# A two-layer decoder trunk in split FP32 on one core: separate banks for one product of the value projection, and another order for its operand sums

## The chip, the cores and the metric

The kernel runs on one core of a Trainium2 chip. The metric is the device time of one launch in microseconds (us). Engines are named as the profile names them: PE multiplies matrices (PEld is its weight load), DVE is the vector engine, ACT the scalar engine, POOL and SP issue DMAs among other things. Every engine works through its own list of instructions in order. PE writes into eight accumulator banks of 128 x 512 FP32, which only DVE and ACT empty.

## The reference

Two post-norm layers; each is one input projection of 512 tokens, three groups of attention heads, gates, an output projection and a layer norm. Cut to what matters:

```python
def hybrid_layer(x, mem, w_in, b_forget, w_mem_kv, w_out, ln_gain, ln_bias):
    h = jnp.einsum('bsd,dn->bsn', x, w_in)            # 512 x 2048 times 2048 x 8278
    (fq, fk, fv, fg, f_logit, dq, dk, dv, dg, iq, ik, iw, mq, mg) = jnp.split(h, offsets, axis=-1)
    cum_logf = jnp.cumsum(jax.nn.log_sigmoid(f_logit + b_forget), axis=1)
    y_fox = fox_attention(heads(fq), heads(fk), heads(fv), cum_logf) * jax.nn.silu(fg)
    # dsa: an indexer scores all keys of a query, the best 128 are kept
    y_dsa = dsa_attention(rope(heads(dq), pos), rope(heads(dk), pos), heads(dv),
                          q_idx, k_idx, w_idx) * jax.nn.silu(dg)
    y_mem = memory_attention(heads(mq), k_mem, v_mem) * jax.nn.silu(mg)
    y = jnp.einsum('bsn,nd->bsd', jnp.concatenate([y_fox, y_dsa, y_mem], axis=-1), w_out)
    return layer_norm(ALPHA * x + y, ln_gain, ln_bias)
```

All arrays are FP32. The change concerns how `fv`, `dv`, `fg` and `dg` (3072 columns of `h`) are computed, and when the best 128 keys are picked.

## The kernel before, in words

**Products.** A number is held as a first part `hi`, rounded by ACT to the format that PE multiplies fast, and a second part `lo = x - hi`, made by DVE (`split`, lines 197 to 199). A product is three matmuls: hi x hi, lo x hi, hi x lo (lines 205 to 207).

**Weights.** They arrive in chunks of 128 x 2048 (1 MB) in three buffers `raw`. A chunk is used in two half-steps. `split_w` turns half a chunk into `whi` (ACT, line 198) and `wlo` (DVE, line 199); there are four buffers of each. At half-step n the program splits the half that half-step n+3 needs, so `whi` of n+3 takes the buffer that PE frees at the end of half-step n-1.

**The value stage.** The 3072 value and gate columns are computed for three pairs of 512-column blocks. For each pair there are seven products in place of eight block products (Strassen's scheme in Winograd's form). The left operands are blocks of x (A11, A12, A22) or sums of them (S1 to S4); the right ones are weight blocks or sums of these (T1 to T4), which lie ready in DRAM, or are made by a DMA that adds a block to a chunk in place (`grow_w`, line 234). A product has two chunks (g = 0 and 1), so four half-steps of twelve matmuls. In each layer first come P1, P7, P2, Q6 and Q4 for the pairs 0, 1 and 2 (`VAL_FIRST`, P2 in two parts around Q6), then Q5 and Q3 for all three (`VAL_SECOND`).

A product accumulates in two banks (for the token halves st = 0 and 1). P1, P7, Q6 and Q4 of a pair share the two banks of chain "a", one accumulating on the other, P2 has chain "b", and Q5 and Q3 share chain "c". When a product's last half-step is issued, `val_out` takes out what stands in its banks: after P1 a copy M1 (ACT, line 804); after P7 the difference to M1, M7 (DVE, line 807); after P2 M1 plus the bank (DVE, line 810); after Q6 minus the bank (ACT, line 814) and M7 minus the bank (DVE, line 817); after Q4, Q5 and Q3 a copy (ACT, line 821). The results go to DRAM by DMAs that POOL issues.

**Operand sums.** `val_operands` is a generator that makes S3 and S2 early, and then waits until the last P7 is through. It then makes S1 for the four feature tiles i = 0 to 3, waits for the last Q6, and makes S4. The sum S2 itself is dropped once it is split (the split holds -S2); so for each tile of S1 or S4 line 767 adds its two parts up again, four additions on half tiles (line 731) bring in the two parts of the x block, ACT makes the first part `vxh` (line 736), and after one yield DVE makes the second part `vxl` (line 741).

**What sets the order.** The program is written out in the order in which the engines get it. A list `active` holds generators like `val_operands`; `tick` resumes each once after a half-step, and those begun with `whole=True` only after a chunk while the value stage runs. In the attention heads all of them go on after each half.

**Key choice.** `top_keys` picks 128 keys a query in 48 rounds on DVE (lines 604 and 605: the largest eight, then strike them out), two rounds a step; 16 rounds each for 256, 384 and 512 keys. It is begun when the last Q6 is issued, and goes on in the rest of the value stage and the first heads. The DSA heads, six heads later, need its result.

Of the kernel before, what the change touches and what calls it, by code (L numbers as in the profile page):

```python
# [70 lines left out]
VAL_FIRST = (("P1", 0), ("P1", 1), ("P7", 0), ("P7", 1), ("P2", 0), ("Q6", 0), ("Q6", 1), ("P2", 1),  # L71
             ("Q4", 0), ("Q4", 1))
VAL_SECOND = (("Q5", 0), ("Q5", 1), ("Q3", 0), ("Q3", 1))
VAL_CHAIN = {"P1": "a", "P7": "a", "Q6": "a", "Q4": "a", "P2": "b", "Q5": "c", "Q3": "c"}
VAL_OPENS = ("P1", "P2", "Q5")
GROWN = {"Q6": ("P7", (0, 0)), "Q4": ("Q6", (1, 0))}


# [79 lines left out]
def kernel(  # L158
# [244 lines left out]

    kmem, vmem, gates, qs, ks, vs = {}, {}, {}, {}, {}, {}
    ys, left = {}, {}
    masks = {}

    def gate(key, ps):

# [187 lines left out]
    def top_keys(l):  # L597
        acc = masks[l]
        for qb in (1, 2, 3):
            b, off, w = PACK[qb]  # L600
            a = acc[b][:, off:off + w]
            for n in range(TOPK // 8):
                m8 = small("m8", 8)
                nc.vector.max(m8, a)
                nc.vector.match_replace(out=a, in_to_replace=m8, in_values=a, imm_value=TAKEN)
                if n % 2:
                    yield 1 + n // 2 % 2 if now[1] == "heads" else 1

            nc.vector.tensor_scalar(a, a, TAKEN / 2, NEG, op0=ALU.is_gt, op1=ALU.mult)

    def attend(l, kind, h):
        key = (kind, h)
# [130 lines left out]
    def val_operands():  # L743
        add, sub = ALU.add, ALU.subtract
        a11, a12, a21, a22 = (0, 0), (0, 1), (1, 0), (1, 1)

        for i in range(4):
            val_sum("S3", i, ((a11, 0, add), (a21, 0, sub), (a11, 1, add), (a21, 1, sub)))
            yield 1
        for i in range(4):  # L750
            val_hi("S3", i)
            val_sum("S2", i, (("S3", 0, add), (a22, 0, add), (a22, 1, add)))
            yield 1
            val_lo("S3", i)
            yield 1
        for i in range(4):
            hi, lo = vleft["S2", i] = slot("vxh", F32R), slot("vxl", F32R)
            nc.scalar.activation(hi, vx["S2", i], AF.Copy, scale=-1.0)
            yield 1
            nc.vector.scalar_tensor_tensor(lo, vx.pop(("S2", i)), -1.0, hi.bitcast(F32),  # L760
                                           op0=ALU.mult, op1=ALU.subtract)
        for name, a, after in (("S1", a11, "P7"), ("S4", a12, "Q6")):
            yield from wait_for(after)
            for i in range(4):
                t = vx["-S2", i] = slot("vx")
                hi, lo = vleft["S2", i] if name == "S1" else minus.pop(i)
                nc.vector.tensor_tensor(t, hi.bitcast(F32), lo.bitcast(F32), op=add)
                val_sum(name, i, (("-S2", 0, add), (a, 0, add), (a, 1, add)), vx.pop(("-S2", i)))
                val_hi(name, i)
                yield 1  # L770
                val_lo(name, i)
            yield 1

    val_done, minus = [], {}

    def wait_for(name):

# [12 lines left out]
    def val_out(name, pair, ps):  # L790


        if pair == PAIRS - 1:
            val_done.append(name)
            for k in [k for k in vleft if k[0] == PRODUCTS[name][1]]:
                operand = vleft.pop(k)
                if name == "Q6":
                    minus[k[1]] = operand
        j = 2 * pair
        for st in range(2):  # L800
            m1, m7 = ("M1", pair, st), ("M7", pair, st)
            if name == "P1":
                vraw[m1] = slot("vraw")
                nc.scalar.activation(vraw[m1], ps[st], AF.Copy)
            elif name == "P7":
                vraw[m7] = slot("vraw")
                nc.vector.tensor_tensor(vraw[m7], ps[st], vraw[m1], op=ALU.subtract)
            elif name == "P2":
                d = vraw.pop(m1)
                nc.vector.tensor_tensor(d, d, ps[st], op=ALU.add)  # L810
                begin(store_v(d, (j, st)), 1)
            elif name == "Q6":
                d = slot("vraw")
                nc.scalar.activation(d, ps[st], AF.Copy, scale=-1.0)
                begin(store_v(d, (j + 1, 2 + st)), 1)
                d = vraw.pop(m7)
                nc.vector.tensor_tensor(d, d, ps[st], op=ALU.subtract)
                begin(store_v(d, (j + 1, st)), 1)
            else:
                d = slot("vraw")  # L820
                nc.scalar.activation(d, ps[st], AF.Copy)
                key = {"Q4": (j, 2 + st), "Q5": (j + 1, 2 + st), "Q3": (j + 1, st)}[name]
                begin(store_v(d, key, name != "Q4"), 1)

    def store_v(t, key, add=False):
        if add:
# [183 lines left out]
    for i, (kind, l, j, col, _) in enumerate(chunks):  # L1010
# [122 lines left out]
        elif kind == "vs":  # L1133
            if col == 1:
                val_out(name, pair, zs)
                if name in ("Q4", "P2", "Q3"):
                    del chains[VAL_CHAIN[name], pair], zs
        elif kind == "small":
            sm = slot("sm")
            nc.scalar.activation(sm, ps, AF.Copy)  # L1140
            r = slice(96, 96 + H_FOX)
            nc.scalar.activation(sm[r], ps[r], AF.Identity, bias=bfc[r, l:l + 1])
            t = index_rope(ps, 64, 0, nc.vector)
            kh2, kl2 = slot("kh2", F32R), slot("kl2", F32R)
            for r in (0, 64):
                nc.scalar.activation(kh2[r:r + 64], t[:64], AF.Copy)
                nc.vector.tensor_tensor(kl2[r:r + 64], t[:64], kh2.bitcast(F32)[:64],
                                        op=ALU.subtract)
            idx["k"] = (kh2, kl2)
            begin(small_work(l, sm))  # L1150
            if l > 0:
                begin(residual_rows(l), last=True)
        elif kind == "iq":
            t = index_rope(ps, P, P, nc.gpsimd)

            for e in range(2):
                s = slot("iqs", F32R)
                r, o = (slice(0, 64), slice(64, 128)) if e == 0 else (slice(64, 128), slice(0, 64))
                c = slice(P, SEQ)
                nc.scalar.activation(s[r, c], t[r, c], AF.Copy)  # L1160
                nc.vector.tensor_tensor(s[o, c], t[r, c], s.bitcast(F32)[r, c], op=ALU.subtract)
                idx["q", 2 * j + e] = s
            if j == 3:
                begin(index_scores(l), 2, last=True, but="vs")
# [12 lines left out]
            now = (l, "values")  # L1177
        if kind == "mg" and j == 0:
            begin(val_operands(), 2, last=True)
        if kind == "vs" and (name, pair, col) == ("Q6", PAIRS - 1, 1):  # L1180
            begin(top_keys(l), whole=True)
        if kind == "vs" and (name, pair, col) == ("Q3", PAIRS - 1, 1):
            chains.clear()
# [113 lines left out]
```

## Time and profile before

| | |
|---|---|
| median of 3 runs | 1982.84 us (1982.15 to 1982.87) |
| profiled execution | 1982.03 us |
| its span, first to last instruction | 1980.2 us |
| PE busy | 1935.7 us, 98% |
| DVE busy | 1367.2 us, 69% |
| ACT busy | 940.8 us, 48% |
| POOL busy | 315.0 us, 16% |
| HBM traffic | 284 GB/s over the span |

The page's slices show PE at nine tenths or more nearly everywhere. A slice is 49.5 us, so a wait of 1 to 3 us is lost in it. The views that matter are the list of PE's waits, the busy time in stretches of equal work (a stretch is given as from:to in us from the span's start, then its length, then busy time and instructions of each engine, the granted PE clock, and the share and rate of the DMA engines), and the instructions in order of time. A few per cent of the matmul records can be missing, and a stretch counts the instructions that cross its edges.

### The profile page before, as it was taken

How to read it: one execution, taken by the hardware profiler on the slowest of the kernel's cores; microseconds unless marked ns; L12 is line 12 of the kernel's file. 1: busy time of each engine (PE TensorE's matmuls, PEld its weight loads, DVE VectorE, ACT ScalarE, POOL GpSimd, SP SyncE). 2: the span in 40 equal slices, each digit the busy share in tenths (PEclk: the TensorE clock that was granted, in tenths of full speed). 3: DMA queues.
4: the chain of work that ended last, by engine and by line, in shares of the span. 5: the costliest groups of instructions: out<-in, count | busy, mean ns of one | idle time of the engine just before them, and what ended most of it. 6: DMA issues, size and time to landing. Idle time of an engine off the chain costs nothing.

```text
span 1980.2 us, 25263 instructions
## 1 busy us (share of the span) xinstructions
PE 1935.7 (98%) x9314; PEld 1639.5 (83%) x9314; DVE 1367.2 (69%) x2291; ACT 940.8 (48%) x1510; POOL 315.0 (16%) x551
## 2 busy tenths in 40 slices
PE   9999999979999999999999999999799999999997
PEld 8998888858888888888899988887588888888886
DVE  6666664578664567778886877655887645667788
ACT  6564454334343444455475644443443444345452
POOL 0121111111122110110142301110112212002101
PEclk9999999989999999999999999999899999999999
DMA  9568788748786667788889953886596866668856
GB/s 370 199 204 248 214 220 225 212 150 255 239 208 184 182 181 253 209 313 308 247 259 349 257 168 119 220 233 165 178 260 225 212 205 181 169 232 248 308 211 153
DMA packets 88057, 444.21 MB, mean 224 GB/s; under 512 B 11504, under 2 KB 23792, under 8 KB 49404
## 3 DMA queue, kind: packets, MB, share of 16 engines
q0 software_dynamic: 27872, 184.59, 37.9%
q1 hardware_dynamic: 60060, 257.99, 36.1%
q8 instruction: 73, 1.20, 0.2%
q14 instruction: 52, 0.43, 0.1%
HBM read 411.06 MB, written 151.02 MB: 284 GB/s over the span
## 4 chain that ended last, share of the span: by engine, by line
PE 90%; DVE 5%; ACT 2%; issue 1%; DMA 0%; SPq 0%; POOL 0%; DVEq 0%; ACTq 0%; POOLq 0%
PE c L207 15%; PE c L205 15%; PE c L206 15%; PE v L206 7%; PE v L207 7%; PE v L205 7%; PE z L206 5%; PE z L205 5%; PE z L207 5%; PE pt L650 1%; ACT whi L198 1%; DVE wlo L199 1%; DVE vx L731 1%; PE po L207 1%; PE po L206 1%
## 5 line engine op out<-in xcount | busy, mean ns | idle before, releaser
L199 DVE TENSOR_TENSOR wlo<-raw,whi 128x1024 fp32r<-128x1024 f32 (+1 forms) x473 | 581.7, 1234 | 275.8 <-ACT whi L198 269.3
L198 ACT ACTIVATE whi<-raw 128x1024 fp32r<-128x1024 f32 (+1 forms) x473 | 495.5, 1053 | 316.6 <-PE v L207 166.1
L205 PE MATMUL c<-xh,whi 128*128 128x512 f32 (+1 forms) x1312 | 502.5, 383 | 0.0
L207 PE MATMUL c<-xh,wlo 128*128 128x512 f32 (+1 forms) x1312 | 498.3, 380 | 0.0
L206 PE MATMUL c<-xl,whi 128*128 128x512 f32 (+1 forms) x1312 | 496.9, 379 | 0.0
L207 PEld LDWEIGHTS c<-xh,wlo 128*128 128x128 f32 x1312 | 246.2, 188 | 42.7
L206 PEld LDWEIGHTS c<-xl,whi 128*128 128x128 f32 x1312 | 246.6, 188 | 40.5
L205 PEld LDWEIGHTS c<-xh,whi 128*128 128x128 f32 x1312 | 246.4, 188 | 39.8
L327 POOL TENSOR_TENSOR seen<-mark,mhalf 128x1 f32<-128x1 f32 x112 | 36.9, 329 | 871.9 <-DVE mark L326 848.9
L206 PE MATMUL z<-wlo,yh 128*128 128x512 f32 (+1 forms) x434 | 167.8, 387 | 1.2 <-DVE wlo L199 1.2
L205 PE MATMUL z<-whi,yh 128*128 128x512 f32 (+1 forms) x434 | 168.1, 387 | 0.0
L207 PE MATMUL z<-whi,yl 128*128 128x512 f32 (+1 forms) x434 | 167.7, 386 | 0.0
L205 PE MATMUL v<-whi,vxh 128*128 128x512 f32 x384 | 150.3, 391 | 5.5 <-ACT whi L198 3.4
L206 PE MATMUL v<-wlo,vxh 128*128 128x512 f32 x384 | 150.3, 391 | 4.9 <-DVE wlo L199 4.9
L207 PE MATMUL v<-whi,vxl 128*128 128x512 f32 x384 | 149.4, 389 | 0.0
L205 PE MATMUL v<-whi,xh 128*128 128x512 f32 x288 | 117.5, 408 | 13.3 <-ACT whi L198 13.3
L206 PE MATMUL v<-wlo,xh 128*128 128x512 f32 x288 | 117.3, 407 | 5.5 <-DVE wlo L199 5.5
L207 PE MATMUL v<-whi,xl 128*128 128x512 f32 x288 | 116.8, 405 | 0.0
L206 PEld LDWEIGHTS z<-wlo,yh 128*128 128x128 f32 x434 | 81.6, 188 | 18.1 <-DVE wlo L199 2.1
L207 PEld LDWEIGHTS z<-whi,yl 128*128 128x128 f32 x434 | 81.5, 188 | 16.6
L205 PEld LDWEIGHTS z<-whi,yh 128*128 128x128 f32 x434 | 81.5, 188 | 16.3
L206 PEld LDWEIGHTS v<-wlo,vxh 128*128 128x128 f32 x384 | 72.1, 188 | 22.8 <-DVE wlo L199 8.2
(208 smaller groups left out, 2895.9 us busy)
## 6 DMA issues: line engine op xcount, KB each, us to landing
raw<-in_wall_dram SPq DMA_DIRECT2D x155, 1024.0 KB, 7.2
sum<-in_wall_dram POOLq DMA_DIRECT2D x56, 1024.0 KB, 9.7
raw<-sum SPq DMA_DIRECT2D x56, 1024.0 KB, 6.3
raw<-in_wall_dram POOLq DMA_DIRECT2D x24, 1024.0 KB, 8.0
v<-vraw POOLq DMA_DIRECT2D x72, 256.0 KB, 5.2
x<-z POOLq DMA_DIRECT2D x32, 256.0 KB, 9.6
vraw<-v SPq DMA_DIRECT2D x96, 64.0 KB, 5.4
vraw<-v SPq DMA_DIRECT2D x24, 256.0 KB, 6.7
```

Source lines behind the costliest of these rows:

```text
L198: nc.scalar.activation(hi, src, AF.Copy)
L199: nc.vector.tensor_tensor(lo, src, hi.bitcast(F32), op=ALU.subtract)
L205: nc.tensor.matmul(ps, ah, bh, start=start, stop=False, skip_group_check=more)
L206: nc.tensor.matmul(ps, ah, bl, start=False, stop=False, skip_group_check=more)
L207: nc.tensor.matmul(ps, al, bh, start=False, stop=stop, skip_group_check=more)
L327: nc.gpsimd.tensor_tensor(seen, mark, mhalf, op=ALU.mult)
L650: nc.tensor.transpose(tp[tb][:, toff + (qb - kt) * P:toff + (qb - kt + 1) * P], pr[b][:, off + kt * P:off + (kt + 1) * P], ident)
L731: nc.vector.tensor_tensor(d, acc, x, op=op)
```

## The change

P1 gets banks of its own (chain "d"), and P7 opens chain "a". So after P7 the bank holds M7 itself, and ACT copies it. After Q6 the bank holds M7 and Q6's product without M1: DVE makes minus the bank minus M1 in one instruction, and then adds this to M7. After Q4 DVE adds M1 to the bank. P2's sum goes to a new buffer, since M1 is needed until Q4.

The sums S2 are kept. S1 is A11 minus S2, S4 is A12 minus S2 (written over S2 for the last use), so the addition of line 767 goes. The generator now makes a sum in one step, and in the next one the second part of the tile before and the first part of this tile. S4's first sum does not wait for Q6; the parts of S4 do.

Key choice is begun when the second chunk of Q5 of pair 0 is issued, five chunks later than before.

```diff
-VAL_CHAIN = {"P1": "a", "P7": "a", "Q6": "a", "Q4": "a", "P2": "b", "Q5": "c", "Q3": "c"}
-VAL_OPENS = ("P1", "P2", "Q5")
+VAL_CHAIN = {"P1": "d", "P7": "a", "Q6": "a", "Q4": "a", "P2": "b", "Q5": "c", "Q3": "c"}
+VAL_OPENS = ("P1", "P7", "P2", "Q5")
+VAL_ENDS = ("P1", "Q4", "P2", "Q3")
...
             nc.scalar.activation(hi, vx["S2", i], AF.Copy, scale=-1.0)
             yield 1
-            nc.vector.scalar_tensor_tensor(lo, vx.pop(("S2", i)), -1.0, hi.bitcast(F32),
+            nc.vector.scalar_tensor_tensor(lo, vx["S2", i], -1.0, hi.bitcast(F32),
                                            op0=ALU.mult, op1=ALU.subtract)
-        for name, a, after in (("S1", a11, "P7"), ("S4", a12, "Q6")):
-            yield from wait_for(after)
-            for i in range(4):
-                t = vx["-S2", i] = slot("vx")
-                hi, lo = vleft["S2", i] if name == "S1" else minus.pop(i)
-                nc.vector.tensor_tensor(t, hi.bitcast(F32), lo.bitcast(F32), op=add)
-                val_sum(name, i, (("-S2", 0, add), (a, 0, add), (a, 1, add)), vx.pop(("-S2", i)))
-                val_hi(name, i)
-                yield 1
-                val_lo(name, i)
-            yield 1
+        yield from wait_for("P7")
+        for n in range(9):
+            if n < 4:
+                val_sum("S1", n, ((a11, 0, add), ("S2", 0, sub), (a11, 1, add)))
+            elif n < 8:
+                val_sum("S4", n - 4, ((a12, 0, add), ("S2", 0, sub), (a12, 1, add)),
+                        vx.pop(("S2", n - 4)))
+            yield 1
+            if n == 4:
+                yield from wait_for("Q6")
+            if n:
+                name, i = (("S1", n - 1), ("S4", n - 5))[n > 4]
                 val_lo(name, i)
+            if n < 8:
+                val_hi(*(("S1", n), ("S4", n - 4))[n > 3])
+            yield 1
...
-            if name == "P1":
-                vraw[m1] = slot("vraw")
-                nc.scalar.activation(vraw[m1], ps[st], AF.Copy)
-            elif name == "P7":
-                vraw[m7] = slot("vraw")
-                nc.vector.tensor_tensor(vraw[m7], ps[st], vraw[m1], op=ALU.subtract)
+            if name in ("P1", "P7"):
+                d = vraw[m1 if name == "P1" else m7] = slot("vraw")
+                nc.scalar.activation(d, ps[st], AF.Copy)
             elif name == "P2":
+                d = slot("vraw")
+                nc.vector.tensor_tensor(d, ps[st], vraw[m1], op=ALU.add)
+                begin(store_v(d, (j, st)), 1)
+            elif name == "Q6":
+                d, e = slot("vraw"), vraw.pop(m7)
+                nc.vector.scalar_tensor_tensor(d, ps[st], -1.0, vraw[m1], op0=ALU.mult,
+                                               op1=ALU.subtract)
+                nc.vector.tensor_tensor(e, e, d, op=ALU.add)
+                begin(store_v(d, (j + 1, 2 + st)), 1)
+                begin(store_v(e, (j + 1, st)), 1)
+            elif name == "Q4":
                 d = vraw.pop(m1)
                 nc.vector.tensor_tensor(d, d, ps[st], op=ALU.add)
-                begin(store_v(d, (j, st)), 1)
-            elif name == "Q6":
-                d = slot("vraw")
-                nc.scalar.activation(d, ps[st], AF.Copy, scale=-1.0)
-                begin(store_v(d, (j + 1, 2 + st)), 1)
-                d = vraw.pop(m7)
-                nc.vector.tensor_tensor(d, d, ps[st], op=ALU.subtract)
-                begin(store_v(d, (j + 1, st)), 1)
+                begin(store_v(d, (j, 2 + st)), 1)
...
-                if name in ("Q4", "P2", "Q3"):
+                if name in VAL_ENDS:
                     del chains[VAL_CHAIN[name], pair], zs
...
-        if kind == "vs" and (name, pair, col) == ("Q6", PAIRS - 1, 1):
+        if kind == "vs" and (name, pair, col) == ("Q5", 0, 1):
             begin(top_keys(l), whole=True)
```

Three places of the built program, in layer 0. First DVE, where the first two tiles of S1 are made (`raw`, `whi`, `wlo` are a weight chunk and its parts, `vx` a sum, `vxh` and `vxl` its parts, `xh` and `xl` the parts of x). Before:

```order
L199 TENSOR_TENSOR wlo_3560<-raw_3402,whi_3559 128x1024
L741 TENSOR_TENSOR vxl_3555<-vx_3548,vxh_3554 128x512
L767 TENSOR_TENSOR vx_3576<-vxh_2681,vxl_2682 128x512
L731 TENSOR_TENSOR vx_3576<-vx_3576,xh_489 128x256
L731 TENSOR_TENSOR vx_3576<-vx_3576,xl_490 128x256
L731 TENSOR_TENSOR vx_3576<-vx_3576,xh_493 128x256
L731 TENSOR_TENSOR vx_3576<-vx_3576,xl_494 128x256
L199 TENSOR_TENSOR wlo_3586<-raw_3438,whi_3585 128x1024
```

And in the change (line numbers have moved on by one to fourteen):

```order
L200 TENSOR_TENSOR wlo_3581<-raw_3442,whi_3580 128x1024
L734 TENSOR_TENSOR vx_3596<-xh_489,vx_2389 128x256
L734 TENSOR_TENSOR vx_3596<-vx_3596,xl_490 128x256
L734 TENSOR_TENSOR vx_3596<-xh_493,vx_2389 128x256
L734 TENSOR_TENSOR vx_3596<-vx_3596,xl_494 128x256
L200 TENSOR_TENSOR wlo_3605<-raw_3442,whi_3604 128x1024
L744 TENSOR_TENSOR vxl_3578<-vx_3554,vxh_3577 128x512
```

Before, every weight half is followed by a whole tile (second part of the one, all additions of the next); now the additions follow one weight half and the second part follows the next, and the first addition reads the kept S2 (`vx_2389`). Second, ACT at the same place. Before:

```order
L736 ACTIVATE vxh_3554<-vx_3548 128x512
L198 ACTIVATE whi_3559<-raw_3402 128x1024
L736 ACTIVATE vxh_3582<-vx_3576 128x512
L198 ACTIVATE whi_3585<-raw_3438 128x1024
L736 ACTIVATE vxh_3608<-vx_3602 128x512
L198 ACTIVATE whi_3614<-raw_3438 128x1024
```

And in the change:

```order
L199 ACTIVATE whi_3561<-raw_3406 128x1024
L739 ACTIVATE vxh_3577<-vx_3554 128x512
L199 ACTIVATE whi_3580<-raw_3442 128x1024
L199 ACTIVATE whi_3604<-raw_3442 128x1024
L739 ACTIVATE vxh_3621<-vx_3596 128x512
L199 ACTIVATE whi_3624<-raw_3602 128x1024
```

Before, a first part of a sum stands ahead of every weight half; now ahead of every second one, and a weight half later than its sum. Third, PE at the end of P1 and the start of P7 of pair 0 (`v` is a bank; `ptm` belongs to a head of the group before, whose last matmuls fall between). Before:

```order
L207 MATMUL v_2618<-whi_2621,xl_572 128x512
L455 MATMUL ptm_2704<-ident,pm_2600 128x128 x2
L455 MATMUL ptm_2704<-ident,pm_2601 128x128 x2
L455 MATMUL ptm_2713<-ident,pm_2600 128x128 x2
L455 MATMUL ptm_2713<-ident,pm_2601 128x128 x2
L205 MATMUL v_2617<-whi_2638,vxh_2270 128x512
```

And in the change:

```order
L208 MATMUL v_2618<-whi_2621,xl_572 128x512
L456 MATMUL ptm_2704<-ident,pm_2600 128x128 x2
L456 MATMUL ptm_2704<-ident,pm_2601 128x128 x2
L456 MATMUL ptm_2713<-ident,pm_2600 128x128 x2
L456 MATMUL ptm_2713<-ident,pm_2601 128x128 x2
L206 MATMUL v_2726<-whi_2638,vxh_2270 128x512
```

P7 used to start in the bank that P1 had left (`v_2617`); now it starts in a new one (`v_2726`).

More of the change, by code (lines that the diff above doesn't have):

```diff
@@ L405 @@
     ys, left = {}, {}
-    masks = {}
+    masks, chosen = {}, set()
     def gate(key, ps):
@@ L609, in top_keys @@
             nc.vector.tensor_scalar(a, a, TAKEN / 2, NEG, op0=ALU.is_gt, op1=ALU.mult)
+        chosen.add(l)
     def attend(l, kind, h):
@@ L621, in attend @@
         if kind == "d":
+            assert l in chosen
             bt = masks[l]
@@ L759, in val_operands @@
             yield 1
-            nc.vector.scalar_tensor_tensor(lo, vx.pop(("S2", i)), -1.0, hi.bitcast(F32),
+            nc.vector.scalar_tensor_tensor(lo, vx["S2", i], -1.0, hi.bitcast(F32),
                                            op0=ALU.mult, op1=ALU.subtract)
-        for name, a, after in (("S1", a11, "P7"), ("S4", a12, "Q6")):
-            yield from wait_for(after)
-            for i in range(4):
-                t = vx["-S2", i] = slot("vx")
-                hi, lo = vleft["S2", i] if name == "S1" else minus.pop(i)
-                nc.vector.tensor_tensor(t, hi.bitcast(F32), lo.bitcast(F32), op=add)
-                val_sum(name, i, (("-S2", 0, add), (a, 0, add), (a, 1, add)), vx.pop(("-S2", i)))
-                val_hi(name, i)
-                yield 1
+        yield from wait_for("P7")
[10 more added lines that the diff above has]
+                name, i = (("S1", n - 1), ("S4", n - 5))[n > 4]
                 val_lo(name, i)
+            if n < 8:
+                val_hi(*(("S1", n), ("S4", n - 4))[n > 3])
             yield 1
-    val_done, minus = [], {}
+    val_done = []
     def wait_for(name):
@@ L795, in val_out @@
             for k in [k for k in vleft if k[0] == PRODUCTS[name][1]]:
-                operand = vleft.pop(k)
-                if name == "Q6":
-                    minus[k[1]] = operand
+                del vleft[k]
         j = 2 * pair
@@ L821, in val_out @@
                 nc.scalar.activation(d, ps[st], AF.Copy)
-                key = {"Q4": (j, 2 + st), "Q5": (j + 1, 2 + st), "Q3": (j + 1, st)}[name]
-                begin(store_v(d, key, name != "Q4"), 1)
+                begin(store_v(d, (j + 1, st + 2 * (name == "Q5")), True), 1)
     def store_v(t, key, add=False):
```

## The prediction

> **What bounds the kernel now.** I read the engines' totals and the chain of waits first, then the list of PE's waits.
>
> ```profile
> span 1980.2 us, 25263 instructions
> PE 1935.7 (98%) x9314; PEld 1639.5 (83%) x9314; DVE 1367.2 (69%) x2291; ACT 940.8 (48%) x1510; POOL 315.0 (16%) x551
> PE 90%; DVE 5%; ACT 2%; issue 1%; DMA 0%; SPq 0%; POOL 0%; DVEq 0%; ACTq 0%; POOLq 0%
> ...
> PE v L205 <- ACT whi L198: 17.1, 9, 3.2
> PE v L206 <- DVE wlo L199: 10.6, 17, 0.8
> PE v L205 <- ACT vraw L804: 2.0, 2, 1.0
> PE z L206 <- DVE wlo L199: 1.2, 2, 0.6
> ```
>
> PE is the bound, so only what PE does not lose any more counts. Three of its waits are in the value stage (`v` is a value bank): 27.7 us for the two parts of a weight half, 2.0 us for the copy after P1 (total, times, longest). PE waits for no DMA. But busy time hides losses at a lowered clock, so the next view takes stretches of equal work, value matmuls alone (from:to, length, PE, PEld, DVE, ACT, POOL busy, PE clock, DMA share, GB/s).
>
> ```profile
> 248.62:306.56 57.94, 54.87 (x240) 44.98 (x241) 3.93 (x6) 2.86 (x5) 3.56 (x7) 1.00 0.87 230
> 306.56:360.96 54.40, 54.40 (x241) 45.06 (x240) 3.93 (x6) 3.60 (x6) 4.37 (x9) 1.00 0.84 232
> 382.72:449.45 66.73, 53.15 (x194) 39.36 (x192) 3.56 (x6) 2.73 (x5) 4.62 (x9) 0.90 0.51 155
> 449.45:503.85 54.40, 54.40 (x241) 44.86 (x239) 0.00 (x0) 5.99 (x10) 8.65 (x11) 1.00 0.88 256
> 1365.77:1432.51 66.74, 53.15 (x193) 39.37 (x192) 3.56 (x6) 2.73 (x5) 4.61 (x9) 0.90 0.51 156
> ```
>
> Pair 1 is the ruler: 240 matmuls in 54.40 us, 0.2267 each, so 2.72 us for a half-step of twelve. The third row runs from P2's first chunk of pair 2 over Q6, Q6, P2, Q4, Q4 and the first two chunks of `VAL_SECOND`: 8 chunks, 192 matmuls, 43.52 us by the ruler, and it takes 66.73. The loss is 23.21 us, and 23.22 in layer 1 (last row): **46.43 together**, much more than the 27.7 of the wait list. Of each, 66.73 - 53.15 = 13.58 is PE idle, and 53.15 - 43.52 = 9.63 is busy time over the ruler. The instructions in order of time show both kinds (bracket: idle before, and who ended it).
>
> ```profile
> 393.47 1.22 DVE L199 TENSOR_TENSOR wlo<-raw,whi 128x1024 fp32r<-128x1024 f32 x1 [1.65 <-ACT whi L198]
> 394.61 0.68 DVE L741 TENSOR_TENSOR vxl<-vx,vxh 128x512 fp32r<-128x512 f32 x1
> 395.21 0.69 DVE L767 TENSOR_TENSOR vx<-vxh,vxl 128x512 f32<-128x512 f32 x1
> 395.93 0.43 DVE L731 TENSOR_TENSOR vx<-vx,xh 128x256 f32<-128x256 f32 x1
> ...
> 397.19 0.42 DVE L731 TENSOR_TENSOR vx<-vx,xl 128x256 f32<-128x256 f32 x1
> 399.25 1.23 DVE L199 TENSOR_TENSOR wlo<-raw,whi 128x1024 fp32r<-128x1024 f32 x1 [1.64 <-ACT whi L198]
> ```
>
> ```profile
> 397.65 0.63 ACT L736 ACTIVATE vxh<-vx 128x512 fp32r<-128x512 f32 x1 [4.21 <-DVE vx L731]
> 398.18 1.04 ACT L198 ACTIVATE whi<-raw 128x1024 fp32r<-128x1024 f32 x1
> ```
>
> ```profile
> 405.06 0.49 PE L205 MATMUL v<-whi,xh 128*128 128x512 f32 x1 [1.73 <-ACT whi L198]
> 406.32 0.65 PE L206 MATMUL v<-wlo,xh 128*128 128x512 f32 x1 [0.77 <-DVE wlo L199]
> 406.77 0.63 PE L207 MATMUL v<-whi,xl 128*128 128x512 f32 x1
> 407.19 0.63 PE L205 MATMUL v<-whi,xh 128*128 128x512 f32 x1
> ...
> 430.76 0.79 PE L205 MATMUL v<-whi,xh 128*128 128x512 f32 x1 [3.19 <-ACT whi L198]
> ```
>
> It is a loop between two engines. DVE splits a weight half, makes one second part and five additions; ACT, idle for 4.21 us, makes the first part of that sum; only then does `whi` of the next half-step run, which stood behind it in ACT's list; then DVE's `wlo`. One round takes 399.25 - 393.47 = 5.78 us and PE eats a half-step in 2.72, so the look-ahead of three half-steps is used up and PE waits twice in a half-step. After the wait it starts matmuls 0.42 us apart (406.77 to 407.19) instead of 0.23: that is the 9.63.
>
> **The change part by part.**
>
> *Sums in steps of their own.* The loop is cut. The first part now comes a weight half later than its sum, so ACT finds the sum ready, and `whi` stands behind at most a 0.63 us operation that does not wait. What is left to check is whether DVE keeps up by its amount of work; the costs are these groups (last columns: busy, mean ns of one, idle before).
>
> ```profile
> L199 DVE TENSOR_TENSOR wlo<-raw,whi 128x1024 fp32r<-128x1024 f32 x199 | 243.6, 1229 | 128.1 <-ACT whi L198 125.4 <-PE v L207 1.6
> L731 DVE TENSOR_TENSOR vx<-vx,xl 128x256 f32<-128x256 f32 x32 | 13.6, 425 | 1.1
> L741 DVE TENSOR_TENSOR vxl<-vx,vxh 128x512 fp32r<-128x512 f32 x12 | 8.2, 682 | 0.0
> L810 DVE TENSOR_TENSOR vraw<-vraw,v 128x512 f32<-128x512 f32 x6 | 3.8, 681 | 0.0
> L760 DVE SCALAR_TENSOR_TENSOR vxl<-vx,vxh 128x512 fp32r<-128x512 f32 x4 | 2.7, 683 | 0.0
> ```
>
> Two half-steps hold two `wlo`, one sum and one second part: 2 x 1.229 + 4 x 0.425 + 0.682 = 4.84 us, under 5.44. From P2's first chunk of pair 2 on there are 14 half-steps with 8 sums, 7 second parts and 8 operations that empty banks: 14 x 1.229 + 32 x 0.425 + 7 x 0.682 + 8 x 0.68 = 17.2 + 13.6 + 4.8 + 5.4 = 41.0 us, against 14 x 2.72 = 38.1. By full durations DVE falls 2.9 us behind; by starts it does not, for a 0.68 us operation lets the next start 0.60 later (394.61 to 395.21) and a `wlo` 1.14 later: 16.0 + 13.4 + 4.2 + 4.8 = 38.4. The cushion is 3 x 2.72 - (1.04 + 1.23) = 5.9 us, so I take no stall: **-46.43 us**. The bounds are that, and that half of the stall stays (first rival).
>
> *The sums kept.* Eight additions of line 767 a layer go, 0.69 us each. They lie in that loop, so their gain is in the 46.43 already.
>
> *P1's own banks.* PE stood idle at the start of P7 of pair 0, until ACT had copied P1's bank:
>
> ```profile
> 261.57 0.50 PE L205 MATMUL v<-whi,vxh 128*128 128x512 f32 x1 [1.00 <-ACT vraw L804]
> ```
>
> P7 now opens a bank that nobody reads, so the two waits of 1.0 us go: **-2.0 us**. In the other pairs the list shows no such wait, so nothing is gained there. No other bank becomes scarcer: by the order the products of a pair never hold more than six of the eight at once.
>
> *What leaves the banks.* After P7 a copy on ACT in place of a subtraction on DVE; after Q6 two operations on DVE in place of one on ACT and one on DVE; after Q4 one on DVE in place of ACT's copy. The trace has no operation of the new form (bank times -1 minus a tile); the nearest rows are an addition with a bank (681 ns, L810) and that instruction without a bank (683 ns, L760), so 0.68. In pairs 0 and 1 this hides: DVE needs 2 x 1.23 + 2 x 0.68 = 3.8 us in the two half-steps around an end, of 5.44. In pair 2 it is counted above. A bank is wanted again two half-steps (5.44 us) after its product's end, which covers both operations. The added copy on ACT is 0.6 us:
>
> ```profile
> L821 ACT ACTIVATE vraw<-v x36: 577/598/601, 305.4 to 1487.1; 128x512 f32<-128x512 f32 x36
> ```
>
> *A new wait.* The last sum of S4 now falls into Q5 of pair 0. Q3 accumulates on Q5's banks, so Q5's copy must be out when Q3 starts; the first bank is complete six matmuls (1.36 us) earlier and the copy takes 0.60, which leaves 0.76. But on ACT that copy stands behind the first part of S4's last tile, which waits for DVE's sum. Laying the queues out by starts the copy ends 0.1 us before Q3 wants its bank, by full durations 1.1 late. The bounds are 0 and 1.1 a layer; I take 0.4, nearer the starts because rows do overlap: **+0.8 us**.
>
> *Weights sooner.* Chunks are now used at 2.72 us a half-step also there, and T4's addition is made by POOL's DMA on a chunk while it waits:
>
> ```profile
> raw<-in_wall_dram POOLq DMA_DIRECT2D x24, 1024.0 KB, 8.0
> ```
>
> In that stretch the DMA engines' share goes from 0.51 to 0.51 x 66.73 / 43.52 = 0.78; pair 1 runs at 0.84 without a wait. By the order, Q4's grown chunk is asked for when a buffer comes free a little over a half-step (some 3.1 us) after P2's first chunk of pair 2 begins, and lands 8.0 later, at 11.1. Q4 begins after four chunks, 21.8, and its split three half-steps before, at 13.6. No cost, with 2.5 us to spare; the bounds are 0 and one landing late by some 2 us a layer.
>
> *Key choice later.* Rounds cost:
>
> ```profile
> L604 DVE MAX8 m<-acc 128x8 f32<-128x512 f32 x16 | 11.0, 690 | 0.3
> L605 DVE MATCH_REPLACE8 acc<-m,acc 128x512 f32<-128x512 f32 x16 | 10.8, 676 | 0.0
> L604 DVE MAX8 m<-acc 128x8 f32<-128x384 f32 x16 | 8.9, 557 | 0.3
> L605 DVE MATCH_REPLACE8 acc<-m,acc 128x384 f32<-128x384 f32 x16 | 8.7, 543 | 0.0
> ```
>
> By the two programs' orders 17 rounds of a layer lay in the heads (16 of 512 keys, one of 384) and 27 do now: ten more, 10 x 1.10 = 11 us of DVE. What hides them is DVE's free time in the heads:
>
> ```profile
> 551.00:565.00 14.00, 14.00 (x72) 12.04 (x71) 10.69 (x24) 5.80 (x13) 1.10 (x3) 1.00 0.83 197
> 592.00:606.00 14.00, 14.00 (x71) 11.70 (x70) 5.25 (x9) 6.11 (x11) 4.41 (x10) 1.00 0.38 140
> ```
>
> In the first of these stretches DVE is at key choice (10.69 of 14.00) and PE is never idle; in the second, six heads on, 8.75 are free. The result is ready 304 matmuls, some 69 us, ahead of the DSA heads. No cost, if the cover holds.
>
> **Sum.** 1982.03 (profiled execution; its span is 1.8 less) - 46.43 - 2.0 + 0.8 = 1934.4; the median is 0.81 over that execution, so **1935.2 us**.
>
> **The rivals.**
>
> *A part of the stall stays.* DVE falls behind when Q6's four bank operations meet S4's sums, and PE waits there for `wlo`. For it: 41.0 us of work in 38.1. Against: the cushion of 5.9, twice the 2.9. If half of a stretch's 23.2 stays, 1935.2 + 23.2 = 1958; with a quarter, 1947.
>
> *The clock is not the waits' doing.* If something else in that stretch lowered it, 9.63 a layer stays: 1935.2 + 19.3 = 1954.5. For it: the trace shows matmuls 0.42 us apart after idle times of 1.73 and 0.77 us, and this stretch has the mean clock 0.80:
>
> ```profile
> 403.00:411.40 8.40, 5.90 (x18) 4.24 (x17) 6.69 (x11) 4.44 (x6) 1.94 (x4) 0.80 0.84 205
> ```
>
> Against: the clock is 1.00 in the three other stretches of layer 0 above, which lack these waits. The Trainium skill, "TensorE: Matmul & The Clock Gate", section "What's actually happening", speaks for this rival: it halves the clock after at least one idle window of about 3.4 us. The trace does not bear that out as a need for one long gap: 1.73 and 0.77 were enough here.
>
> *Slower: key choice on PE's path.* In the heads, DVE also splits what PE multiplies next, and each step of two rounds stands ahead of it for 2 x 1.10 to 2 x 1.37 us. 27 rounds are 16 x 1.366 + 11 x 1.10 = 34.0 us a layer; all of it exposed gives 1935.2 + 68 = 2003. It is slower than before from 47.6 / 2 = 23.8 us exposed a layer. Against: 17 such rounds, 23 us, ran in the heads with no wait of PE.
>
> *Nothing changes.* The weights set that stretch's pace, PE's waits only pass from `whi` to the chunk: about 1982. Against: the share of 0.51, lower than in every undisturbed stretch.
>
> **How the numbers follow.** Forecast 0.74 (its own range 1933 to 1939: the new wait at 0 or 1.1 a layer, a late chunk); a part stays 0.14; clock 0.03; slower 0.04; nothing 0.03; the last 0.02 for a gain beyond it. A measurement of this kernel can tell about 0.2%, 4 us, from no change. All cases but two are faster: faster 0.93, same 0.03, slower 0.04. The range goes from 1932.5 to 1948, which takes in the quarter of the stall that may stay.
>
> **What would show it.** The stretch from P2's first chunk of pair 2 takes 43.5 to 45 us in both layers at clock 1.00; `wlo` starts there 2.7 us apart on average; the waits for `whi` and `wlo` in value banks, and for the copy after P1, are gone from the list; at most 1.1 us for Q5's copy is new. Waits for `wlo` after Q6 mean the first rival; a clock under 1.00 with no wait the second; a wait in the heads for a split behind L604 or L605 the third; a wait for a chunk the fourth.

## The result, and the profile after

| | before | after |
|---|---|---|
| median | 1982.49 us (1981.36 to 1982.87, 4 runs) | 1933.56 us (1932.22 to 1933.81, 4 runs) |
| ratio | | 0.9753 (95%: 0.9736 to 0.9770) |
| profiled execution, its span | 1982.03, 1980.2 | 1932.22, 1930.5 |
| value stage, layer 0 and 1 | 255.23, 255.29 | 230.77, 230.77 |

The forecast was 1935.2. In the page after, PE's busy time falls by 19.7 us and the span by 49.7; in the list of PE's waits (total, times, longest) all but 0.2 us of the waits in value banks is gone.

```profile
span 1930.5 us, 25233 instructions
PE 1916.0 (99%) x9314; PEld 1632.5 (85%) x9314; DVE 1361.3 (71%) x2287; ACT 935.8 (48%) x1498; POOL 318.2 (16%) x551
...
PE warm L305 <- POOL mhalf L307: 1.4, 1, 1.4
PE z L207 <- DVE wlo L200: 1.2, 2, 0.6
PE c L208 <- DVE wlo L200: 0.3, 1, 0.3
PE v L207 <- DVE wlo L200: 0.2, 1, 0.2
```

The same stretches of equal work, value matmuls alone (from:to, length, PE, PEld, DVE, ACT, POOL busy, clock, DMA share, GB/s): pair 0 and the late stretch of layer 0, and the late stretch of layer 1.

```profile
248.52:305.21 56.69, 54.86 (x241) 44.99 (x242) 2.94 (x5) 2.14 (x4) 3.30 (x6) 1.00 0.89 231
...
381.36:424.88 43.52, 43.52 (x193) 36.05 (x192) 3.93 (x6) 1.20 (x2) 4.64 (x9) 1.00 0.78 242
...
1339.89:1383.41 43.52, 43.52 (x194) 36.04 (x192) 3.93 (x6) 1.20 (x2) 4.63 (x9) 1.00 0.78 241
```

The late stretch takes 43.52 us in both layers, the ruler's value to the last digit, at clock 1.00: 23.21 and 23.22 us are gone. Pair 0 lost 57.94 - 56.69 = 1.25, and 1.30 in layer 1 (57.99 before). Together 49.0 of the 49.7 us of the span; most of the rest lies behind the start of the last matmul (11.9 us before, 11.2 after), and no run here asks why.

Why the stall is gone is seen on DVE and ACT where S1's tiles are made (start, duration; in brackets the idle time before and who ended it).

```profile
390.87 1.23 DVE L200 TENSOR_TENSOR wlo<-raw,whi 128x1024 fp32r<-128x1024 f32 x1 [0.88 <-ACT whi L199]
392.01 0.42 DVE L734 TENSOR_TENSOR vx<-xh,vx 128x256 f32<-128x256 f32 x1
...
393.60 1.22 DVE L200 TENSOR_TENSOR wlo<-raw,whi 128x1024 fp32r<-128x1024 f32 x1
394.74 0.68 DVE L744 TENSOR_TENSOR vxl<-vx,vxh 128x512 fp32r<-128x512 f32 x1
396.31 1.23 DVE L200 TENSOR_TENSOR wlo<-raw,whi 128x1024 fp32r<-128x1024 f32 x1 [0.88 <-ACT whi L199]
```

```profile
392.50 1.06 ACT L199 ACTIVATE whi<-raw 128x1024 fp32r<-128x1024 f32 x1 [1.67 <-PE v L208]
393.71 0.63 ACT L739 ACTIVATE vxh<-vx 128x512 fp32r<-128x512 f32 x1
```

`wlo` now starts 2.7 us after the last one, no longer 5.8; `vxh` finds its sum ready; and what ACT waits for is PE, which frees the buffers. The splits are again as far ahead as the four buffers let them be.

That picture holds for the first three sums. From Q6 on, the last sum of S1 and the four of S4 come later: in layer 0 ACT waits for them again, 2.81, 3.04, 1.94, 2.29 and 1.32 us, with `whi` behind the first part.

```profile
407.48 0.63 ACT L739 ACTIVATE vxh<-vx 128x512 fp32r<-128x512 f32 x1 [3.04 <-DVE vx L734]
408.02 2.00 ACT L199 ACTIVATE whi<-raw 128x1024 fp32r<-128x1024 f32 x2
```

But DVE has no idle time from the split at 396.31 to the end of the stretch: each `whi` is there when DVE comes to its split. So these waits do not close the loop again; what DVE's amount of work costs there is taken from how far the splits are ahead.

How far ahead can be read exactly: the end of a `wlo` against the first matmul that uses it. I call that distance the lead. It is 5.8 us on the rows above (5.9 by the prediction), and smallest right after Q6, whose four bank operations and a sum stand between two splits:

```profile
397.45 0.69 DVE L817 SCALAR_TENSOR_TENSOR vraw<-v,vraw 128x512 f32<-128x512 f32 x1
...
400.11 0.42 DVE L734 TENSOR_TENSOR vx<-xh,vx 128x256 f32<-128x256 f32 x1
...
401.70 1.22 DVE L200 TENSOR_TENSOR wlo<-raw,whi 128x1024 fp32r<-128x1024 f32 x1
...
407.36 1.22 DVE L200 TENSOR_TENSOR wlo<-raw,whi 128x1024 fp32r<-128x1024 f32 x1
```

```profile
411.51 0.39 PE L207 MATMUL v<-wlo,xh 128*128 128x512 f32 x1
```

The `wlo` that starts at 407.36 ends at 408.58, and PE uses it at 411.51: 2.93 us, in layer 1 2.94. The other tight place is Q5's copy on ACT, behind S4's last first part:

```profile
422.08 0.63 ACT L739 ACTIVATE vxh<-vx 128x512 fp32r<-128x512 f32 x1 [1.32 <-DVE vx L734]
422.62 1.05 ACT L199 ACTIVATE whi<-raw 128x1024 fp32r<-128x1024 f32 x1
423.72 0.60 ACT L828 ACTIVATE vraw<-v 128x512 f32<-128x512 f32 x1
```

```profile
424.88 0.39 PE L206 MATMUL v<-whi,vxh 128*128 128x512 f32 x1
```

The copy ends at 424.32, and Q3's first matmul into that bank starts at 424.88 without a wait: 0.56 us to spare.

### The profile page after: what moved, and what is told of

It reads as the page before. It is cut to its first block, busy times and chain, and to the rows that moved or that the text cites. A ratio compares the mean times of both kernels' runs of the same rounds, so it can differ in the third digit from the quotient of the medians.

```text
span 1930.5 us, 25233 instructions
## 1 busy us (share of the span) xinstructions
PE 1916.0 (99%) x9314; PEld 1632.5 (85%) x9314; DVE 1361.3 (71%) x2287; ACT 935.8 (48%) x1498; POOL 318.2 (16%) x551
## 4 chain that ended last, share of the span: by engine, by line
PE 96%; DVE 2%; ACT 1%; DMA 0%; issue 0%; SPq 0%; POOL 0%; DVEq 0%; POOLq 0%
PE c L208 15%; PE c L206 15%; PE c L207 15%; PE v L208 9%; PE v L206 9%; PE v L207 9%; PE z L207 5%; PE z L208 5%; PE z L206 5%; PE pt L653 1%; PE po L208 1%; PE po L207 1%; PE po L206 1%; PE ix L575 1%; PE ix L574 1%; PE s L206 1%
## 5 line engine op out<-in xcount | busy, mean ns | idle before, releaser
L206 PE MATMUL v<-whi,xh 128*128 128x512 f32 x288 | 112.1, 389 | 0.0
L207 PE MATMUL v<-wlo,xh 128*128 128x512 f32 x288 | 112.1, 389 | 0.0
L208 PE MATMUL v<-whi,xl 128*128 128x512 f32 x288 | 112.1, 389 | 0.0
```

The costliest lines, as they stand in the source:

```text
L206: nc.tensor.matmul(ps, ah, bh, start=start, stop=False, skip_group_check=more)
L207: nc.tensor.matmul(ps, ah, bl, start=False, stop=False, skip_group_check=more)
L208: nc.tensor.matmul(ps, al, bh, start=False, stop=stop, skip_group_check=more)
```

## The experiments

The theory: the stall was a loop through ACT's list (the weight half's first part behind a sum's first part that waits for DVE), the wait at P7 is a matter of its own, and the slow clock followed from the waits. The rivals: DVE's amount of work set the stall; a tile needs two half-steps; the banks or the key choice carry part of the gain; the clock has another cause. In each run the losses of a layer are its value stage against the one after, 230.77 us. The diffs are shortened: `...` and lines in brackets stand for code that is left out. Runs 3 and 5 also let the first sum of S4 wait for Q6, as the kernel before does.

**1. The banks alone.** The kernel before, with chain "d" and the operations that go with it.

```diff
-VAL_CHAIN = {"P1": "a", "P7": "a", ...
+VAL_CHAIN = {"P1": "d", "P7": "a", ...      # and val_out, VAL_OPENS, VAL_ENDS of the change
```

> The kernel before with the change's banks and what empties them, and nothing else (old sums, old steps, key choice early). Theory (the two gains are separate): the two waits at the start of P7 go, about 2.3 us with the restarts; the late stretch keeps its 66.7 us a layer and gets up to four more DVE operations of 0.68 in a loop in which DVE is idle 1.65 us a round, so 0 to 2.7 us a layer more: 1980 to 1984. Rival (the shared bank holds back the late stretch as well, through what empties it): the stretch shrinks by several us a layer, 1975 or less.

Measured 1979.98, ratio to before 0.9985 (0.9976 to 0.9994). The wait on line 804's copy is off the list, pair 0 takes 56.69 as after; the late stretch is as long as ever:

```profile
382.11:449.09 66.98, 53.48 (x193) 39.98 (x192) 3.93 (x6) 1.20 (x2) 4.66 (x9) 0.87 0.48 145
```

So the banks give 1.25 to 1.30 us a layer, and with their added DVE operations the stall that is still there is 0.25 us longer.

**2. The rest without the banks.**

```diff
-VAL_CHAIN = {"P1": "d", "P7": "a", ...
+VAL_CHAIN = {"P1": "a", "P7": "a", ...      # and val_out, VAL_OPENS, VAL_ENDS of before
```

> The change without P1's own banks: banks and what empties them as before, the kept S2, the new steps and the late key choice stay. Theory (the gains are separate): only the wait at the start of P7 of pair 0 comes back, 1.25 us a layer by the profiles: 1933.6 + 2.5 = 1936 (1935 to 1938). Rival (the other operations after Q6 and Q4 matter in the late stretch): a shorter or longer late stretch than 43.5 us, by 1 us a layer or more.

Measured 1935.50 (ratio 0.9762, 0.9747 to 0.9776), 1.9 over the change. The late stretch is 43.52 us in both layers, pair 0 58.02, and in the value stages one line of PE's waits is back:

```profile
PE v L206 <- ACT vraw L810: 2.0, 2, 1.0
```

So the two gains are separate, but for the 0.25 us of run 1: each comes in the stretch where it was expected, whether the other is there or not.

**3. The old steps with the kept sum.** Everything of the change but its steps.

```diff
+            val_hi(*order[n])
             yield 1
-            if n: ...
-            if n < 8: val_hi(...)
-            yield 1
+            val_lo(*order[n])
```

> The change with the steps of before: sum and first part in one half-step, the second part in the next, a tile every half-step; the kept S2, the banks and the late key choice stay. Theory (ACT's list order closes the loop): the round loses only the addition of line 767, 5.78 - 0.72 = 5.06 us against PE's 2.72, so 23.2 - 8 x 0.7 = 17.6 us a layer stay: 1933.6 + 35 = about 1969 (1962 to 1974). Rival (the amount of DVE work sets it, and the kept sum is what helps): 3.44 us a half-step by starts is 2.9 behind over four tiles, within the lead of 5.9: 1934 to 1940.

Measured 1959.50 (0.9882, 0.9868 to 0.9895), between the two, and below the theory's range. The stretch:

```profile
382.15:438.83 56.68, 48.99 (x193) 37.72 (x192) 3.93 (x6) 1.20 (x2) 4.66 (x9) 0.94 0.60 184
```

PE idle in it is 56.68 - 48.99 = 7.69 against 13.58 before: 5.9 less, the eight additions of 0.72 that the theory took off. But the busy time over the ruler also fell, from 9.63 to 5.47, since fewer waits slow fewer matmuls. That second part was not in the estimate. The loop itself is as it was, now with a `wlo` every 5.06 us, and DVE still idle for 1.64 us of it, until `whi` is there:

```profile
395.31 1.23 DVE L200 TENSOR_TENSOR wlo<-raw,whi 128x1024 fp32r<-128x1024 f32 x1 [1.65 <-ACT whi L199]
...
400.37 1.22 DVE L200 TENSOR_TENSOR wlo<-raw,whi 128x1024 fp32r<-128x1024 f32 x1 [1.64 <-ACT whi L199]
```

So the amount of work is not what closes it.

**4. One tile every half-step, the first part late.**

```diff
+            if n > 1: val_lo(*order[n - 2])
+            if n == 5: yield from wait_for("Q6")
+            if 0 < n < 9: val_hi(*order[n - 1])
             (sum of tile n)
             yield 1
```

> The change, but a tile every half-step: in one half-step the second part of the tile two back, the first part of the tile before, and the sum of this tile. So ACT's first part never waits for a sum of its own half-step, and DVE's work is as dense as in the kernel before less line 767. Theory (the order on ACT decides): S1's four tiles cost 2.9 us of the lead of 5.9; S4's four fall together with Q6's and P2's bank operations, 4 x 0.72 + 2.7 + 1.3 = 6.9, 1 more than the lead: 0 to 3 us a layer, 1933.6 to 1940. Rival (what helps is that a tile has two half-steps): as with the old steps, 1962 to 1974.

Measured 1934.08 (0.9753, 0.9740 to 0.9766), no different from the change. The stretch:

```profile
382.03:426.30 44.27, 43.83 (x194) 35.96 (x192) 3.92 (x6) 1.20 (x2) 4.66 (x9) 1.00 0.79 244
```

The same density on DVE that stalled in run 3 by 13 us a layer stalls by 0.75 here. A tile does not need two half-steps; it needs its first part behind a weight half and not in its sum's half-step.

**5. Two half-steps a tile, the first part with its sum.** The reverse of it.

```diff
             (sum of tile n)
+            val_hi(*order[n])
             yield 1
             val_lo(...)
-            if n < 8: val_hi(...)
             yield 1
```

> The change with two half-steps a tile, but the first part in the half-step of its sum, so that the next weight half's first part stands on ACT behind one that waits for that sum. Theory (the order on ACT decides): one round for two half-steps is 1.14 (wlo) + 1.70 (sum) + 0.55 (vxh) + 1.04 (whi) + 1.14 (wlo) + 0.60 (second part) and hand-overs = 6.3 us against 5.44, 0.85 behind a tile; 8 tiles 6.8, bank operations 5.2, less the lead of 5.9: about 6 us a layer, 1946 (1940 to 1952). Rival (two half-steps a tile is all that was needed): 1933 to 1936, no wait for whi.

Measured 1954.91 (0.9858, 0.9843 to 0.9873): the rival falls, and the theory was 9 us short. DVE is idle for `whi` again in each tile, as long as in the kernel before:

```profile
391.21 1.23 DVE L200 TENSOR_TENSOR wlo<-raw,whi 128x1024 fp32r<-128x1024 f32 x1 [1.65 <-ACT whi L199]
```

PE's waits say where the time goes:

```profile
PE v L206 <- ACT vraw L826: 7.1, 2, 3.6
PE v L207 <- DVE wlo L200: 5.8, 10, 0.8
PE v L206 <- ACT whi L199: 3.0, 5, 0.6
```

In the late stretches the waits for weight halves are 3.9 us a layer (the rest of their list lies at the start of the kernel). Another 3.6 are Q5's copy, the "new wait" of the prediction, which the expectation had left out. With what slows PE after the waits the layers lose 9.55 and 10.90 us.

**6. Key choice at its old place.**

```diff
-        if kind == "vs" and (name, pair, col) == ("Q5", 0, 1):
+        if kind == "vs" and (name, pair, col) == ("Q6", PAIRS - 1, 1):
```

> The change with key choice begun at the last Q6, as before: in the five chunks after it two rounds of 256 keys a chunk stand on DVE, about 1.7 us a chunk. Theory (lead): in the change the lead of wlo over PE is 2.93 us at its smallest, just after Q6, and grows by about 1 us a chunk from there; with 1.7 more a chunk it falls by 0.7 a chunk instead and comes near 0: 0 to 3 us a layer, 1933.6 to 1940. Rival (the later key choice is what makes room for the sums): 1945 or more. Third (its place does not matter at all): 1933.6 and a smallest lead above 2.

Measured 1954.87 (0.9858, 0.9842 to 0.9874): 21.3 us over the change. Here my theory failed and the rival's number held.

```profile
PE v L206 <- ACT vraw L828: 8.9, 2, 4.5
PE v L207 <- DVE wlo L200: 6.4, 8, 1.8
```

The rounds put 1.8 us a chunk on DVE just after Q6, where the lead was smallest; it reached 0 after two chunks' rounds, where the estimate had reckoned with a slow fall over five chunks. And the largest wait is again Q5's copy:

```profile
431.84 0.63 ACT L739 ACTIVATE vxh<-vx 128x512 fp32r<-128x512 f32 x1 [3.77 <-DVE vx L734]
432.37 1.04 ACT L199 ACTIVATE whi<-raw 128x1024 fp32r<-128x1024 f32 x1
433.32 1.06 ACT L828 ACTIVATE vraw<-v 128x512 f32<-128x512 f32 x2
```

```profile
433.95 0.80 PE L206 MATMUL v<-whi,vxh 128*128 128x512 f32 x1 [4.46 <-ACT vraw L828]
434.54 0.63 PE L207 MATMUL v<-wlo,vxh 128*128 128x512 f32 x1
434.97 0.63 PE L208 MATMUL v<-whi,vxl 128*128 128x512 f32 x1
```

Key rounds, then the last sum, on DVE; then `vxh`, `whi` and only then the copy on ACT; then PE, at half the clock. The last half-step before Q3, with the wait at its end, and the first one of Q3 lose 6.7 and 2.6 us of the layer's 11.3.

**7. The copy on DVE.** The kernel of run 6, with Q5's copy of pair 0 by DVE.

```diff
+                if (name, pair) == ("Q5", 0):
+                    nc.vector.tensor_copy(d, ps[st])
```

> The change with key choice begun at the last Q6 (the run that lost 21 us), and the copy of Q5's two banks of pair 0 made by DVE instead of ACT; all else alike. Theory (the place on ACT: Q5's copy stands behind the first part of S4's last tile, so DVE's delay reaches PE there first, 4.46 us a layer, and a slow clock after it): on DVE the copy stands ahead of the key rounds and that sum, so the wait falls to 0 to 1.2 us, some of it comes back as waits for a weight half, and the run gains 8 to 13 us: 1942 to 1947. Rival (DVE is behind by that much whatever stands where): the time is lost at the next weight half instead, 1952 or more.

Measured 1957.43 (0.9873, 0.9856 to 0.9889), no gain; the rival's number held. But the run does not tell the two apart, because I had the place wrong: the copy stands on DVE behind the key rounds, the sum and two splits, so it waited for the same work, 5.95 us in place of 4.46.

```profile
PE v L206 <- DVE vraw L829: 11.9, 2, 5.9
```

**8. Early key choice, one tile every half-step.** Runs 4 and 6 together: the same work for DVE, but S4 is through well before Q5's copy.

> Key choice begun at the last Q6, and a tile of S1 and S4 every half-step (first part a half-step behind its sum). DVE has the same work as in the run with early key choice alone, but S4's last first part is through eight ACT instructions before Q5's copy, so that copy waits for no sum. Theory (4.46 us a layer and the slow clock after it were lost at that copy; DVE itself had more than 6 us in hand right after it): the wait at the start of Q3 goes; S4's four half-steps hold 21.1 us of DVE's work against 10.9 and a lead of 5.9, so PE waits about 4.3 us a layer for weight halves, with the clock 5 to 7.5: 1943 to 1949. Rival (DVE's amount of work alone sets the loss, wherever its order lets it show): 1953 or more.

Measured 1946.61 (0.9814, 0.9798 to 0.9831), in the theory's range, 8.3 us below run 6. No wait for the copy is left; the largest is one for a weight half, 3.4 us.

```profile
PE v L207 <- DVE wlo L200: 8.0, 7, 3.4
```

So of the 21.3 us that early key choice costs, some 8 go with the copy's place on ACT, and the other 13 with DVE's work coming too dense after Q6. The split is rough, since this run also moves S4's work closer to Q6.

**9. More work, same order.** Each second part of S1 and S4 is written twice in layer 0 and four times in layer 1.

```diff
+                for _ in range((1, 3)[l]):
+                    nc.vector.tensor_tensor(lo, vx[name, i], hi.bitcast(F32), op=ALU.subtract)
                 val_lo(name, i)
```

> The change with more work on DVE and the same order: each second part of S1 and S4 is written twice in layer 0 (one more operation of 0.68 us a tile, as long as the addition of line 767) and four times in layer 1 (three more). Theory (lead): layer 0: two half-steps hold 4.56 + 0.60 by starts, under 5.44, the smallest lead goes from 2.9 to about 1.5 and the stretch stays at 43.5 us; layer 1: 6.36 against 5.44; DVE's work over 14 half-steps 38.4 + 14.4 = 52.8 against 38.1 + 5.9, so about 9 us of stall and some half-clock: stretch 52 to 56. Rival (the kept sum was needed): layer 0 stalls by 3 us or more.

One execution, 1950.26. The late stretches:

```profile
382.44:428.13 45.69, 43.68 (x193) 35.85 (x191) 3.93 (x6) 1.23 (x3) 4.40 (x8) 1.00 0.73 229
1344.86:1398.78 53.92, 45.16 (x194) 35.41 (x192) 3.92 (x6) 1.23 (x3) 4.39 (x8) 0.99 0.62 192
```

In layer 1 the stretch lies in the expected 52 to 56, but by luck: 4.81 of its 10.40 us over the ruler are a wait for Q5's copy, which the expectation did not have. In layer 0 the smallest lead was 1.53, as expected, and no `wlo` was late; yet PE waited 2.01 us, for Q5's copy, and half the clock followed: 3.9 us of the layer. Here the rival's number held. An operation as long as line 767 in each tile of the new order would thus cost some 4 us a layer, so the kept sum is needed there too; and what the change has in hand is the 0.56 us before Q3, not the lead of 2.9.

**10. Single delays.** One `wlo` written N times more, in stretches that have no wait; two kernels with six delays each, one execution of each.

```diff
+            for _ in range(DOSES.get(chunks[i][:4], 0)):
+                nc.vector.tensor_tensor(lo, raw[i][:, :1024], hi.bitcast(F32), op=ALU.subtract)
```

> The change with six single delays in stretches that have none: at one weight half its second part is written again N times (1.14 us each by starts, 1.23 by full duration). Layer 0: pair 1, P7's second chunk N = 4, Q4's second chunk N = 6; pair 2, P7's second chunk N = 7. Layer 1: the same places N = 8, 5, 10. Lead 5.87 us. Expected waits of PE by starts: N = 4 and 5 none, 6: 1.0, 7: 2.1, 8: 3.3, 10: 5.5. Theory on the clock (a lone wait lowers it as the waits of the stall did): after waits of 1.0 and 2.1 us matmuls 0.43 us apart for some us, each wait costing 2 to 4 us more than its idle time. Rival (only a long gap does, about 3.4 us): nothing beyond the idle time for N = 6 and 7, a slower clock for N = 10 and perhaps 8.

> The single delays again, two sizes at three places each: N = 6 (waits of about 1.6 us) at pair 1 P7 and pair 2 P7 of layer 0 and pair 1 Q4 of layer 1, N = 7 (about 2.8 us) at pair 1 Q4 of layer 0 and pair 1 P7 and pair 2 P7 of layer 1. Theory (the clock goes by the idle share of a window of time that runs by itself): N = 6 keeps the full clock at all three, N = 7 differs from place to place. Rival (a fixed limit on the gap between 1.6 and 2.8): no slow matmul for N = 6, slow ones at all three for N = 7.

Seen in the first (1957.17): waits of 0 (N = 4), 0.33 (5), 1.58 (6), 2.85 (7), 4.10 (8) and 6.62 us (10), 1.25 us a step: written again to the same place an operation costs about its full duration of 1.23, and the estimate by starts was low. After 1.58 the clock stayed; after 4.10 PE went on at half clock; after 2.85 the clock was halved 1.0 us later. In the second (1956.22) three waits of 1.58 and 1.59 changed nothing, behind one N = 7 whose chunk came late too PE waited 5.87 us and went on at half clock, and the two others waited alike and went apart, as the theory had it:

```profile
1296.04 0.79 PE L209 MATMUL v<-wlo,vxh 128*128 128x512 f32 x1 [2.85 <-DVE wlo L237]
1296.63 0.63 PE L210 MATMUL v<-whi,vxl 128*128 128x512 f32 x1
1297.05 0.63 PE L208 MATMUL v<-whi,vxh 128*128 128x512 f32 x1
...
1358.31 0.50 PE L209 MATMUL v<-wlo,vxh 128*128 128x512 f32 x1 [2.84 <-DVE wlo L237]
1358.64 0.39 PE L210 MATMUL v<-whi,vxl 128*128 128x512 f32 x1
1358.87 0.40 PE L208 MATMUL v<-whi,vxh 128*128 128x512 f32 x1
```

Matmuls 0.42 us apart after the one, 0.23 after the other. So a wait does halve the clock, and there is no fixed limit on its length: where in time it falls decides too.

The granted clock shows how. Within each run all its changes lie on one grid with steps of 3.41 us. These are the steps around the two waits (all of PE's matmuls; the clock is the third number from the end):

```profile
1291.91:1295.32 3.41, 1.28 (x6) 0.74 (x4) 3.31 (x4) 1.06 (x1) 0.00 (x0) 1.00 0.00 0
1295.32:1298.73 3.41, 2.69 (x6) 2.15 (x7) 3.41 (x4) 0.00 (x0) 0.11 (x1) 0.50 0.02 5
...
1353.35:1356.76 3.41, 2.11 (x10) 1.42 (x8) 3.34 (x3) 1.32 (x2) 0.00 (x0) 1.00 0.25 50
1356.76:1360.17 3.41, 1.86 (x8) 1.56 (x9) 3.38 (x4) 0.00 (x0) 0.48 (x1) 1.00 0.00 0
```

The first wait put 2.13 us of idle time into one step (3.41 - 1.28), and the next step ran at half clock; the second was cut into 1.30 and 1.55. In the value stages of all thirteen traces, every one of the 26 full-clock steps with 2.01 us or more of PE idle was followed by half clock, none with 1.72 or less was, and of nine between 1.73 and 1.93 two were, both in run 3; what decides there stays open.

## Why the prediction was right

*What bounds, and the loss.* The 46.43 us came out whole: both late stretches are at the ruler. That the loop ran through ACT's list is shown by two pairs that keep DVE's work and its density and move a tile's two parts: 13.2 us a layer in run 3 against 0.75 in run 4, and 9.55 and 10.90 in run 5 against none in the change.

*DVE keeps up.* 2.9 behind by full durations, 5.9 of lead: measured 5.82 going down to 2.93. The step held in its result, but not in its picture, and that both numbers are 2.9 is luck. DVE does not lose it evenly over 14 half-steps; it loses 2.66 at once at Q6's bank operations (397.45 to 400.11), has 4.65 again behind the last sum, and 5.6 in Q3 of pair 0. The reason given with it, that ACT finds the sum ready and `whi` stands behind an operation that does not wait, failed from Q6 on (waits of 1.3 to 3.0 us); there it is the lead that pays.

*P1's banks: mis-sized.* The term was 2.0 from the list of waits; it measured 2.55 (57.94 and 57.99 to 56.69 twice). The list counts a wait from the end of the last matmul before it; without a wait the next matmul starts ahead of that end. After the change P7's first one starts at 260.23, 0.79 us after the eight `ptm` matmuls begin, which are 1.04 us long: 0.25 on top of the 1.00 of the list. The stretches hold that. The same mistake in small that the prediction avoided in the stall.

*The new wait: mis-sized.* 0.8 in the sum, 0 measured, with 0.56 to spare; the reckoning by starts (0.1 to spare) was the nearer. The place was right: in runs 5, 6 and 9 PE waits there for 2.0 to 4.8 us. With 2.55 and 0 in the sum the forecast would have been 1933.9; the two errors point the same way, so they did not hide each other.

*Weights sooner.* It held: the DMA share of the late stretch is 0.78, as reckoned, and PE waits for no chunk.

*Key choice: a gap.* Its cover in the heads held. The stretch that was 592 to 606 lies 24.5 us earlier now, DVE is busy 10.69 us in it where it was 5.25, PE is never idle there, and PE's list has no wait for a split in a head:

```profile
567.50:581.50 14.00, 14.00 (x70) 11.73 (x69) 10.69 (x21) 6.17 (x11) 4.83 (x10) 1.00 0.47 168
```

But the step priced only what the move may cost. What it saves, the prediction never asked; run 6 measured 21.3 us. At its old place key choice would have taken near half the gain, which is the first rival (a part of the stall stays) in size, but in mechanism only in part: its waits for `wlo` after Q6 were 3.0 us a layer, beside 4.5 for Q5's copy.

*The clock.* Its rival is out: clock 1.00 in the late stretches once the waits are gone. But two readings of the prediction say too much. "That is the 9.63" puts all of that time on slow matmuls: by the granted clock PE was busy for 12.83 us at half clock in that stretch, which loses 6.4; the other 3.2 were lost at full clock, where a lone wait of 1.59 us cost 1.88 (a half-step of 4.60 in place of 2.72 in run 10). So the rival's price was some 12.8 us for both layers, not 19.3. And that 1.73 and 0.77 us "were enough here" is so only where both fell into one step of the grid: 2.50 us of idle time from 403.10 to 406.51, and half clock from 406.51 on. The same two waits a round earlier lay in two steps, and the clock stayed. A lone wait of 1.6 us did nothing at four places. The Trainium skill, "TensorE: Matmul & The Clock Gate", section "What's actually happening", has the clock follow how busy PE was over a free-running window of some 3.4 us; that its effect depends on the moment agrees with runs 5 and 10, where waits of 3.56 and 2.85 us halved it at one place and not at another. That a whole idle window is needed does not: 2.01 us (run 9) and 2.85 were enough.

## What to carry to other kernels

In an in-order engine's list, put nothing that waits for another engine's work of the same step ahead of what the bottleneck needs next; where a tile's parts stood was worth about 10 us a layer here (run 5 against the change), one operation more in each tile 4. Price a moved step on both sides, what it meets at the new place and what it left free at the old. Measure a loss as a stretch against equal work, since the list of waits showed 29.7 us of 49.0, and look for the least time to spare on each list that PE waits for: the lead of the weights was 2.9 us, but a copy with 0.56 gave way first.

## What was not expected of the hardware

The clock after a wait: 0.33 and 1.6 us without effect, 2.0 to 3.6 with or without, from 4.1 on always half in these runs; after a single wait PE was busy at half clock for 2.8 to 6.1 us. What decided was the idle time inside one step of 3.41 us: 2.01 or more halved the next step, 1.72 or less never did, and a step at half clock was followed by another if it held 0.71 us of idle time or more. A wait of 2.85 us so cost 3.2 us in one place and 6.0 in another (half-steps of 5.87, and of 8.09 and 3.34, against 2.72). Repeating an operation on the same output took 1.25 us each where different ones follow each other after 1.14.
